# First norm of a decoder trunk: two weight chunks transferred ahead of the second and third tile of x, and split one token tile earlier

## The chip, the cores and the metric

The kernel runs on one core of one Trainium2 chip. The metric is the device time of one execution in microseconds; the time before is the median of three runs. A core has five engines, each with an instruction stream of its own that it works off in order: TensorE (PE, matrix products, into PSUM), VectorE (DVE), ScalarE (ACT), GpSimd (POOL) and SyncE (SP), which here issues all transfers between DRAM and SBUF. The engines wait for each other through semaphores.

## The reference, cut to what matters

The program is a decoder trunk of two residual layers (attention in the first, retention in the second) and a final norm, all in float32, for 512 tokens of width 1024. The change touches only the beginning: the first RMS norm of x and the first of many projections with the wide matrix `even_w_in`.

```python
def rms_norm(x, g):
    xf = x.astype(f32)
    y = xf * lax.rsqrt(jnp.mean(xf * xf, axis=-1, keepdims=True) + EPS)
    return (y * g.astype(f32)).astype(x.dtype)

def even_layer(x, g_norm, w_in, b_f, w_out):
    z = rms_norm(x, g_norm) @ w_in
    ...
    return x + y @ w_out
```

## The kernel before

The 512 tokens are four tiles of 128 (`NT`), one token to a partition, in `xres`. The width 1024 is eight tiles of 128 (`KT`).

**Products.** Each operand of a product is split into a high and a low part (line 140, `split`): ScalarE copies the value rounded to the fast matmul type, VectorE subtracts that copy from the value. A product is then three matmuls (line 210, `three`; lines 211 to 213): high by high, high by low, low by high. So TensorE's L211 needs only ScalarE's halves, L212 VectorE's half of the one operand and L213 that of the other.

**Weights.** They come in chunks of 512 KB: `load_next` (line 163) takes the next chunk of `plan` and issues its transfer into a raw buffer `w_raw`, of which there are three; `split_next` (line 170) splits the oldest loaded chunk in two halves (`w_h` on ScalarE, `w_l` on VectorE) and calls `load_next` for another. The first two chunks, 512 rows by 256 columns each, are the two halves of the first projection's weights. Here they are called w0 and w1, and the third, fourth and so on w2, w3.

**First norm.** SyncE issues the gain row, the first tile of x and the identity matrix (lines 87 to 89), then from line 707 on the other three tiles of x, with a `load_next` behind the second tile and one behind the third. TensorE spreads the gain row over the partitions (line 717) and runs a few warm-up matmuls on data of no meaning (`warm_up`, line 704). For each tile, `stats` (line 720) has ScalarE square and sum it (L723) and take the root (L724), VectorE the reciprocal (L726), and VectorE or GpSimd four small steps (L725, L727 to L730); `norm` (line 733) scales the tile in two halves on VectorE (L736); `transpose_tile` (line 148) turns it in two halves of four 128x128 blocks on TensorE (L153, `ps_xt`) and splits each half on the way out of PSUM (`xT`, on ScalarE and VectorE: "evacuation" and "low half" below). The statistics of tile t+2 are written behind the norm of tile t+1.

**What sets the order.** Inside the norm's block the instructions of ScalarE and VectorE stand among themselves as the code has them (`manual_schedule`), as GpSimd's do in the whole program. All else is placed by a scheduler, by its own estimate of when operands are ready: TensorE's and SyncE's order, and on ScalarE and VectorE what belongs to the projections, such as the split of w2, which `weights` (line 201) calls; the scheduler may set it between the norm's instructions. Each engine works through its finished list and stops at the first instruction whose data is missing.

**First projection.** `proj_tokens` with `by_tile` (line 237) goes tile by tile: for each of the four tiles 12 matmuls with w0 and 12 with w1, 96 in all, named `pt`. The next projection (`pf`, line 217) uses w2 and w3 and needs all four tiles.

Of the kernel before, what the change touches and what calls it, by code (L numbers as in the profile page):

```python
# [60 lines left out]
def trunk(ctx: ExitStack, tc, x, even_norm, even_w_in, even_b_f, even_w_out,  # L61
# [78 lines left out]
    def split(hi, lo, src, scale=1.0):  # L140

        act.activation(hi, src, AF.Copy, scale=scale)  # L142
        if isinstance(scale, float) and scale == 1.0:
            dve.tensor_tensor(lo, src, r32(hi), ALU.subtract)  # L144
        else:
            dve.scalar_tensor_tensor(lo, src, scale, r32(hi), ALU.mult, ALU.subtract)  # L146

    def transpose_tile(t, xn):
        for q in range(2):
            ps = ps_t.tile([P, 4, P], F32, tag="t", name="ps_xt")  # L150
            for k in range(4):
                kt = 4 * q + k
                pe.transpose(ps[:, k, :], xn[:, kt * P:(kt + 1) * P], ident)  # L153
            dst = xT[:, :, 4 * q:4 * q + 4, t * P:(t + 1) * P]
            split(dst[:, 0], dst[:, 1], ps)
# [7 lines left out]
    def load_next():  # L163
        if plan:
            src, *how = plan.pop(0)
            raw = wp.tile([P, src.shape[0] // P, src.shape[1]], F32, tag="raw", name="w_raw")
            dma(out=raw, in_=src.rearrange("(k p) c -> p k c", p=P))
            loaded.append((raw, *how))

    def split_next():  # L170
        if loaded:
            raw, de, tiles, kt0 = loaded.pop(0)
            shape = list(raw.shape)
            if tiles:
                h, l = tiles(shape)
            else:

                n, at = (16, 0) if de == "f" else (0, 8 if de == "v" else 0)
                h, l = (wp.tile([P, WCH], F32R, tag=tag, name=name)[:, at:at + 1024 + n * shape[1]].rearrange(
                    "p (k c) -> p k c", k=shape[1]) for tag, name in (("wh", "w_h"), ("wl", "w_l")))  # L180
            src, h_, l_ = raw, h, l
            if de == "f":
                fw = late["fw"].pop(0)
                split(h[:, :, 256:], l[:, :, 256:], fw)
                h_, l_ = h[:, :, 0:256], l[:, :, 0:256]
            elif de is True:
                src = raw.rearrange("p k (f two) -> p k two f", two=2)
                h_, l_ = (z.rearrange("p k (two f) -> p k two f", two=2) for z in (h, l))
            if kt0 is not None:
                for k in range(shape[1]):  # L190
                    split(h_[:, k], l_[:, k], src[:, k], scale=gain1[:, kt0 + k:kt0 + k + 1])
            else:
                n = shape[1] // 2
                for i in range(2):
                    sl = slice(i * n, (i + 1) * n)
                    split(h_[:, sl], l_[:, sl], src[:, sl])
            ready.append((h, l))
            count["split"] += 1
        load_next()
# [190 lines left out]
    with ExitStack() as l0:  # L390
# [311 lines left out]
        def warm_up(n, a):  # L702
            for _ in range(n):
                pe.matmul(warm, lhsT=ident, rhs=a, start=True, stop=True)

        xn = [qp.tile([P, D], F32, tag="q", name="xn") for _ in range(NT)]
        dma(out=xres[:, 1, :], in_=xsrc[:, 1, :])
        load_next()
        dma(out=xres[:, 2, :], in_=xsrc[:, 2, :])
        load_next()  # L710
        dma(out=xres[:, 3, :], in_=xsrc[:, 3, :])
        ones = ap_.tile([1, P], F32, tag="tmp", name="ones", bufs=1)
        pool.memset(ones, 1.0)
# [5 lines left out]
        with tc.manual_schedule(engines={mybir.EngineType.Activation, mybir.EngineType.DVE}):  # L719
            def stats(t, eng):  # L720

                ss, v, sd, r, e = (sm.tile([P, 1], F32, tag=n, name=n) for n in ("ss", "var", "sd", "rs", "re"))
                act.activation(xn[t], xres[:, t, :], AF.Square, accum_out=ss)  # L723
                act.activation(sd, ss, AF.Sqrt, bias=eps, scale=1.0 / D)  # L724
                eng.tensor_scalar(v, ss, 1.0 / D, EPS, ALU.mult, ALU.add)  # L725
                dve.reciprocal(r, sd)  # L726
                eng.tensor_tensor(e, r, v, ALU.mult)  # L727
                eng.tensor_tensor(e, e, r, ALU.mult)
                eng.tensor_scalar(e, e, -0.5, 1.5, ALU.mult, ALU.add)
                eng.tensor_tensor(r, r, e, ALU.mult)  # L730
                return r

            def norm(t, r):
                for h in range(2):
                    hs = slice(h * H, (h + 1) * H)
                    dve.scalar_tensor_tensor(xn[t][:, hs], xres[:, t, hs], r, gain0[h], ALU.mult, ALU.mult)  # L736

            norm(0, stats(0, dve))
            r = stats(1, pool)
            for t in range(NT):  # L740
                transpose_tile(t, xn[t])
                if t == 0:
                    warm_up(8, xn[0][:, 0:P])
                if t + 1 < NT:
                    norm(t + 1, r)
                if t < 2:
                    split_next()
                    r = stats(t + 2, pool)
        load_constants()
        for f in G[0]["proj"]:  # L750
# [179 lines left out]
```

## Time and profile before

| | |
|---|---|
| time, median of three runs | 1008.73 us (1007.95 to 1008.86) |
| the profiled execution | 1007.98 us |
| its span, first to last instruction | 1006.0 us |
| DMA, mean over the span | 99 GB/s |
| VectorE busy, share of the span | 64% |

All times inside an execution count from the start of its span. A line of the time line gives start, duration, engine, line of code, operation, output and inputs, the count of merged instructions and, in brackets, how long the engine had been idle and what ended that. A line of the waits gives the total wait in us, how often, and the longest. A line of the table by stretches gives the stretch, its length, the busy time of PE, PE's weight loads, DVE, ACT and POOL with their instruction counts, the granted clock, the share of the DMA engines and GB/s. The stage at issue is the first 30 us:

```profile
PEclk9999999999999999999999999999999999999999
DMA  7554776534556694336433223222212321332112
GB/s 207 114 138 78 156 83 104 145 97 98 135 105 111 118 94 129 77 72 134 77 103 117 74 89 122 84 84 84 84 64 84 105 83 64 87 103 84 64 42 83
```

Each digit or number stands for a fortieth of the span, 25 us; the first is the stage of the change, where transfers are at their densest.

### The profile page before, as it was taken

Reading aid. Unit: us, or ns where it says so; the run is one execution under the profiler, and the core shown is the slowest. Engines: PE = TensorE matmul, PEld = TensorE weight load, DVE = VectorE, ACT = ScalarE, POOL = GpSimd, SP = SyncE. Lnnn points to the kernel's source line nnn. Section 1 sums busy time; section 2 is a strip of 40 time slices with the busy share of each in tenths; the row PEclk is TensorE's granted clock in tenths of the full one; section 3 lists DMA queues with packets and bytes.
Section 4 is the critical chain, followed back from the end, with each engine's and each line's share of the span. In section 5 each row is a group of like instructions: output and inputs, shape, how many; then the busy total and the mean of one; then the engine's idle time right before and its main releaser. Section 6 shows DMA issues by size and latency. Waiting matters only on the chain.

```text
span 1006.0 us, 14334 instructions
## 1 busy us (share of the span) xinstructions
PE 984.2 (98%) x5150; PEld 834.5 (83%) x5150; DVE 644.5 (64%) x1427; ACT 496.9 (49%) x1029; POOL 230.9 (23%) x331
## 2 busy tenths in 40 slices
PE   8999999999999999999999999999999999999997
PEld 6888898888888988988987789787888888888875
DVE  6458576685676676666668755667547834784485
ACT  6366465555645645654658654253433343334333
POOL 1011444445344441211213100202101300130021
PEclk9999999999999999999999999999999999999999
DMA  7554776534556694336433223222212321332112
GB/s 207 114 138 78 156 83 104 145 97 98 135 105 111 118 94 129 77 72 134 77 103 117 74 89 122 84 84 84 84 64 84 105 83 64 87 103 84 64 42 83
DMA packets 74295, 99.98 MB, mean 99 GB/s; under 512 B 6369, under 2 KB 49633, under 8 KB 74098
## 3 DMA queue, kind: packets, MB, share of 16 engines
q1 hardware_dynamic: 74226, 99.09, 42.3%
q8 instruction: 40, 0.66, 0.3%
q14 instruction: 29, 0.24, 0.1%
HBM read 84.36 MB, written 2.13 MB: 86 GB/s over the span
## 4 chain that ended last, share of the span: by engine, by line
PE 85%; DVE 5%; ACT 3%; issue 2%; DMA 2%; POOL 2%; SPq 0%; DVEq 0%; POOLq 0%; ACTq 0%
PE pf L211 10%; PE pf L212 10%; PE pf L213 10%; PE po L213 6%; PE po L211 5%; PE po L212 5%; PE pw L212 5%; PE pw L213 5%; PE pw L211 5%; PE pt L211 3%; PE pt L213 3%; PE ps_pt L553 3%; PE pt L212 3%; PE ps_o L566 2%; PE ps_s L539 2%
## 5 line engine op out<-in xcount | busy, mean ns | idle before, releaser
L211 PE MATMUL pf<-xT,w_h 128*128 128x512 f32 x512 | 202.0, 394 | 0.0
L213 PE MATMUL pf<-xT,w_l 128*128 128x512 f32 x512 | 200.5, 392 | 0.0
L212 PE MATMUL pf<-xT,w_h 128*128 128x512 f32 x512 | 200.2, 391 | 0.0
L144 DVE TENSOR_TENSOR w_l<-w_raw,w_h 128x512 fp32r<-128x512 f32 x190 | 138.7, 756 | 52.9 <-ACT w_h L142 41.2
L142 ACT ACTIVATE w_h<-w_raw 128x512 fp32r<-128x512 f32 x190 | 111.9, 624 | 90.9 <-PE pf L212 40.4
L546 POOL TENSOR_SCALAR pi<-pi,st 128x512 f32<-128x512 f32 (+3 forms) x128 | 74.8, 586 | 348.6 <-DVE st L545 311.6
L213 PEld LDWEIGHTS pf<-xT,w_l 128*128 128x128 f32 x512 | 96.1, 188 | 21.0
L212 PEld LDWEIGHTS pf<-xT,w_h 128*128 128x128 f32 x512 | 96.2, 188 | 17.9
L211 PEld LDWEIGHTS pf<-xT,w_h 128*128 128x128 f32 x512 | 96.2, 188 | 17.8
L146 DVE SCALAR_TENSOR_TENSOR w_l<-w_raw,small,w_h 128x256 fp32r<-128x256 f32 (+1 forms) x136 | 86.2, 669 | 33.1 <-ACT w_h L142 32.9
L142 ACT ACTIVATE w_h<-w_raw,small 128x256 fp32r<-128x256 f32 (+1 forms) x136 | 73.0, 596 | 66.5 <-PE pw L213 24.4
L142 ACT ACTIVATE pth<-ps_pt 128x512 fp32r<-128x512 f32 (+3 forms) x128 | 55.2, 431 | 85.4 <-PE ps_pt L553 78.9
L212 PE MATMUL pw<-w_l,xT 128*128 128x512 f32 x224 | 87.3, 390 | 1.2 <-DVE w_l L146 1.2
L211 PE MATMUL pw<-w_h,xT 128*128 128x512 f32 x224 | 88.0, 393 | 0.1
L213 PE MATMUL pw<-w_h,xT 128*128 128x512 f32 x224 | 87.3, 390 | 0.0
L544 ACT ACTIVATE pi<-pi,st 128x512 f32<-128x512 f32 (+3 forms) x128 | 71.4, 558 | 27.4 <-DVE st L542 26.5
L211 PE MATMUL pt<-w_h,xT 128*128 128x256 f32 x288 | 81.5, 283 | 1.5 <-ACT w_h L142 1.5
L212 PE MATMUL pt<-w_l,xT 128*128 128x256 f32 x288 | 80.8, 280 | 0.0
L213 PE MATMUL pt<-w_h,xT 128*128 128x256 f32 x288 | 80.5, 280 | 0.0
L843 POOL TENSOR_TENSOR yn<-yn,gate 128x512 f32<-128x512 f32 x16 | 21.8, 1364 | 248.4 <-DVE yn L842 178.8
L333 DVE TENSOR_TENSOR xres<-po,xres 128x512 f32<-128x512 f32 x88 | 59.8, 683 | 26.8 <-PE po L213 26.8
L144 DVE TENSOR_TENSOR ptl<-ps_pt,pth 128x512 fp32r<-128x512 f32 (+3 forms) x128 | 62.1, 487 | 14.8 <-ACT pth L142 12.6
(185 smaller groups left out, 2019.0 us busy)
## 6 DMA issues: line engine op xcount, KB each, us to landing
w_raw<-in_even_w_in_dram SPq DMA_DIRECT2D x64, 512.0 KB, 5.6
w_raw<-in_odd_w_in_dram SPq DMA_DIRECT2D x48, 512.0 KB, 3.6
w_raw<-in_even_w_out_dram SPq DMA_DIRECT2D x16, 512.0 KB, 4.4
w_raw<-in_odd_w_out_dram SPq DMA_DIRECT2D x16, 512.0 KB, 3.5
qb<-qa SPq DMA_DIRECT2D x32, 128.0 KB, 3.0
qb<-qa SPq DMA_DIRECT2D x16, 256.0 KB, 3.2
qa<-qa SPq DMA_DIRECT2D x32, 128.0 KB, 2.5
cs<-c_dram SPq DMA_DIRECT2D x16, 256.0 KB, 3.6
```

The costliest lines, as they stand in the source:

```text
L142: act.activation(hi, src, AF.Copy, scale=scale)
L144: dve.tensor_tensor(lo, src, r32(hi), ALU.subtract)
L146: dve.scalar_tensor_tensor(lo, src, scale, r32(hi), ALU.mult, ALU.subtract)
L211: pe.matmul(ps, lhsT=ah, rhs=bh, start=first, stop=False)
L212: pe.matmul(ps, lhsT=ah, rhs=bl, start=False, stop=False)
L213: pe.matmul(ps, lhsT=al, rhs=bh, start=False, stop=last)
L333: dve.tensor_tensor(xr, ps, xr, ALU.add)
L539: pe.matmul(ps[:, 0:n], lhsT=q[:, 1, qs], rhs=k[:, 0:n], start=False, stop=True)
L544: act.activation(pi[:, 0:n], pi[:, 0:n], AF.Exp, bias=st[:, 0:1], scale=-1.0, accum_out=st[:, 1:2])
L546: pool.tensor_scalar(pi[:, 0:n], pi[:, 0:n], st[:, 2:3], 1.0, ALU.mult, ALU.mult)
L553: pe.transpose(pt[:, (i - j) * P:(i - j + 1) * P], hs["p"][i][:, j * P:(j + 1) * P], ident)
L843: pool.tensor_tensor(yn, yn, r["g"][:, i, :], ALU.mult)
```

## The change

Two edits. The two `load_next` calls move ahead of the second and the third tile of x; and the two `split_next` calls in the norm move forward: w0's split ahead of the loop, in front of tile 0's evacuation, and w1's into the loop's first pass, in front of the statistics of the third tile. The splits also carry the `load_next` calls for w2 and w3 with them.

```diff
         xn = [qp.tile([P, D], F32, tag="q", name="xn") for _ in range(NT)]
+        load_next()
         dma(out=xres[:, 1, :], in_=xsrc[:, 1, :])
         load_next()
         dma(out=xres[:, 2, :], in_=xsrc[:, 2, :])
-        load_next()
         dma(out=xres[:, 3, :], in_=xsrc[:, 3, :])
...
             norm(0, stats(0, dve))
             r = stats(1, pool)
+            split_next()
             for t in range(NT):
                 transpose_tile(t, xn[t])
                 if t == 0:
                     warm_up(8, xn[0][:, 0:P])
                 if t + 1 < NT:
                     norm(t + 1, r)
+                if t == 0:
+                    split_next()
                 if t < 2:
-                    split_next()
                     r = stats(t + 2, pool)
```

SyncE's list, the issues of the first transfers (`xres` is a tile of x, `w_raw` a weight chunk, `dil` a mask table), before and then after:

```order
L707 DMA xres<-in_x_dram 128x1024
L167 DMA w_raw<-in_even_w_in_dram 128x4x256
L709 DMA xres<-in_x_dram 128x1024
L167 DMA w_raw<-in_even_w_in_dram 128x4x256
L711 DMA xres<-in_x_dram 128x1024
L167 DMA w_raw<-in_even_w_in_dram 128x4x256
L404 DMA dil<-in_dil_dram 128x512
L167 DMA w_raw<-in_even_w_in_dram 128x4x256
```

```order
L167 DMA w_raw<-in_even_w_in_dram 128x4x256
L708 DMA xres<-in_x_dram 128x1024
L167 DMA w_raw<-in_even_w_in_dram 128x4x256
L710 DMA xres<-in_x_dram 128x1024
L711 DMA xres<-in_x_dram 128x1024
L167 DMA w_raw<-in_even_w_in_dram 128x4x256 x2
L404 DMA dil<-in_dil_dram 128x512
```

w0 and w1 have each passed one tile of x, the second and the third; w3 has passed `dil`.

ScalarE's list from the square of the second tile on (L723 a square, L724 its root, `xT` an evacuation, `w_h` half a split of a chunk), before and then after:

```order
L723 ACTIVATE xn,ss<-xres 128x1024
L724 ACTIVATE sd<-ss,small 128x1
L142 ACTIVATE xT<-ps_xt 128x4x128 x2
L142 ACTIVATE w_h<-w_raw 128x512 x2
L723 ACTIVATE xn,ss<-xres 128x1024
L724 ACTIVATE sd<-ss,small 128x1
L142 ACTIVATE xT<-ps_xt 128x4x128 x2
L142 ACTIVATE w_h<-w_raw 128x512 x2
L723 ACTIVATE xn,ss<-xres 128x1024
L142 ACTIVATE w_h<-w_raw 128x512
L724 ACTIVATE sd<-ss,small 128x1
L142 ACTIVATE w_h<-w_raw 128x512
```

```order
L723 ACTIVATE xn,ss<-xres 128x1024
L724 ACTIVATE sd<-ss,small 128x1
L142 ACTIVATE w_h<-w_raw 128x512 x2
L142 ACTIVATE xT<-ps_xt 128x4x128 x2
L142 ACTIVATE w_h<-w_raw 128x512 x2
L723 ACTIVATE xn,ss<-xres 128x1024
L724 ACTIVATE sd<-ss,small 128x1
L142 ACTIVATE xT<-ps_xt 128x4x128
L142 ACTIVATE w_h<-w_raw 128x512
L142 ACTIVATE xT<-ps_xt 128x4x128
L723 ACTIVATE xn,ss<-xres 128x1024
L142 ACTIVATE w_h<-w_raw 128x512
```

w0's split now stands ahead of the first tile's evacuation, w1's ahead of the third tile's square, and the first half of w2's, placed by the scheduler, between the two evacuations of the second tile. VectorE's low halves follow in the same order, but for the norm of the second tile, which stands ahead of w1's.

TensorE's list around the last tile's transposes (`xn_116` is that tile; `pt0` are the products of the first two tiles, `pt1` of the last two), before and then after:

```order
L213 MATMUL pt0_283<-w_h_189,xT_81 128x256
L153 MATMUL ps_xt_263<-ident_82,xn_116 128x128 x4
L211 MATMUL pt0_283<-w_h_226,xT_81 128x256
L212 MATMUL pt0_283<-w_l_227,xT_81 128x256
L153 MATMUL ps_xt_270<-ident_82,xn_116 128x128 x4
L213 MATMUL pt0_283<-w_h_226,xT_81 128x256
```

```order
L213 MATMUL pt1_284<-w_h_165,xT_81 128x256
L153 MATMUL ps_xt_263<-ident_82,xn_116 128x128 x4
L211 MATMUL pt1_284<-w_h_165,xT_81 128x256
L212 MATMUL pt1_284<-w_l_166,xT_81 128x256
L153 MATMUL ps_xt_270<-ident_82,xn_116 128x128 x4
```

Before, the last transposes stand behind 36 of the 96 `pt` matmuls, half way through the second tile's; after, behind 57, in the third tile's.

## The prediction

> **What bounds the kernel now.** I read the page first, for the engine that sets the end, then TensorE's waits, then the first 30 us instruction by instruction, since the change stays inside them.
>
> ```profile
> PE 984.2 (98%) x5150; PEld 834.5 (83%) x5150; DVE 644.5 (64%) x1427; ACT 496.9 (49%) x1029; POOL 230.9 (23%) x331
> PE 85%; DVE 5%; ACT 3%; issue 2%; DMA 2%; POOL 2%; SPq 0%; DVEq 0%; POOLq 0%; ACTq 0%
> ```
>
> TensorE (PE) is busy for 98% of the span and carries 85% of the chain that ended last. Little but TensorE's idle time can be won or lost. The table by stretches (us, then each engine's busy time and instruction count) says where that lies:
>
> ```profile
> 11.84:21.47 9.63, 7.29 (x53) 6.16 (x53) 8.67 (x17) 7.84 (x16) 2.36 (x10) 1.00 0.85 216
> 21.47:29.39 7.92, 7.92 (x69) 7.92 (x70) 4.20 (x7) 2.96 (x5) 0.00 (x0) 1.00 0.57 117
> 29.39:1003.00 973.61, 959.57 (x4994) 813.68 (x4992) 627.83 (x1395) 480.50 (x998) 227.12 (x309) 1.00 0.42 96
> ```
>
> From 11.84 (warm-up matmuls over) to 21.47 TensorE idles 2.34 of 9.63 us; from 21.47 to 29.39, when the first `pf` matmul starts, not at all; afterwards 14.04 us in 973.61, spread out. In those 9.63 us VectorE (8.67) and ScalarE (7.84) are the full ones. So the question is **when the first `pf` matmul starts**: whatever it shifts by, all behind it shifts by, as nothing later is moved by the change. Who was waited for up to 21.6 us:
>
> ```profile
> PE pt L211 <- ACT w_h L142: 1.5, 2, 0.8
> PE ps_xt L153 <- DVE xn L736: 0.7, 1, 0.7
> ```
>
> Two waits on a weight split, one on a normalised tile. The change aims at the first two; the price is paid by the tiles.
>
> **Landings.** I write x1, x2, x3 for the second to fourth tile of x, w0, w1, w2 for the weight chunks. SyncE's issues (start, us), then the time from issue to landing, of the same five in that order:
>
> ```profile
> 2.01 0.43 SPq L707 DMA_DIRECT2D xres<-in_x_dram  x1
> 2.49 0.43 SPq L167 DMA_DIRECT2D w_raw<-in_even_w_in_dram  x1
> 2.96 0.51 SPq L709 DMA_DIRECT2D xres<-in_x_dram  x1
> 3.51 0.43 SPq L167 DMA_DIRECT2D w_raw<-in_even_w_in_dram  x1
> 3.99 1.76 SPq L711 DMA_DIRECT2D xres<-in_x_dram  x1
> ```
>
> ```profile
> xres<-in_x_dram SPq DMA_DIRECT2D x1, 512.0 KB, 4.8
> w_raw<-in_even_w_in_dram SPq DMA_DIRECT2D x1, 512.0 KB, 9.4
> xres<-in_x_dram SPq DMA_DIRECT2D x1, 512.0 KB, 10.1
> w_raw<-in_even_w_in_dram SPq DMA_DIRECT2D x1, 512.0 KB, 11.1
> xres<-in_x_dram SPq DMA_DIRECT2D x1, 512.0 KB, 11.9
> ```
>
> They land at 6.8 (x1), 11.9 (w0), 13.1 (x2), 14.6 (w1) and 15.9 (x3): in the order of issue. All are 512 KB, yet w0 came 5.1 us after x1 and x2 only 1.2 after w0.
>
> **The change, part by part.** No instruction and no byte is added or removed. Three things move.
>
> (1) x1 goes behind w0, x2 behind w1. x0 landed at about 4.7 (first row below). If w0 keeps its 5.1 us it lands at 9.8, and x1 1.2 later, as x2 did: **11.0**. Bounds: late, 11.9, where the pair w0 and x1 as a whole was done before; early, 7.5, when each takes no longer than x3 behind w1 (1.3 to 1.4 us). I take 11.0, nearest to how w0 itself behaved. w1 then lands 1.5 behind x1 or later, by 13.3; x2 by 14.6, x3 at 15.9, w2 behind x3 at about 17.2 (by 17.54 in any case, where its split ran): the same five in front of the same place.
>
> (2) On ScalarE the square of x1 stands ahead of everything else and now waits 4 us longer. Queued behind it: both halves of w0's split, tile 0's evacuation, w1's split, the square of x2. ScalarE's rows of before give the steps:
>
> ```profile
> 4.70 1.06 ACT L723 ACTIVATE xn<-xres 128x1024 f32<-128x1024 f32 x1 [2.48 <-DMA xres<-in_x_dram]
> 6.87 1.06 ACT L723 ACTIVATE xn<-xres 128x1024 f32<-128x1024 f32 x1 [0.63 <-DMA xres<-in_x_dram]
> 13.11 1.06 ACT L723 ACTIVATE xn<-xres 128x1024 f32<-128x1024 f32 x1
> 14.50 1.06 ACT L142 ACTIVATE xT<-ps_xt 128x512 fp32r<-128x512 f32 x2
> 15.46 1.15 ACT L142 ACTIVATE w_h<-w_raw 128x512 fp32r<-128x512 f32 x2
> 16.50 1.05 ACT L723 ACTIVATE xn<-xres 128x1024 f32<-128x1024 f32 x1
> 17.54 0.62 ACT L142 ACTIVATE w_h<-w_raw 128x512 fp32r<-128x512 f32 x1
> 18.06 0.28 ACT L724 ACTIVATE sd<-ss,small 128x1 f32<-128x1 f32 x1
> ```
>
> Start to start: square with its root 1.39 (13.11 to 14.50), two evacuations 0.96, two split halves 1.04, a half 0.52. After: square x1 11.0, w0 12.4, tile 0 13.4, w1 14.4, square x2 15.4 (before 13.11, where x2's landing held it), free at 16.8. Tile 1's two evacuations now stand on both sides of w2's first half, so the square of x3 follows at about 18.5 (before 16.50) and its root at 18.5 + 1.56 = 20.0 (before 18.06). The chain of tile 3 is 2.0 us late on ScalarE.
>
> (3) VectorE's order follows, and there the delay is met by slack. Its rows, with the last step on GpSimd:
>
> ```profile
> 13.09 1.29 DVE L144 TENSOR_TENSOR w_l<-w_raw,w_h 128x512 fp32r<-128x512 f32 x2
> 14.62 0.17 DVE L726 RECIPROCAL rs<-sd 128x1 f32<-128x1 f32 x1 [0.25 <-ACT sd L724]
> 15.76 0.19 POOL L730 TENSOR_TENSOR rs<-rs,re 128x1 f32<-128x1 f32 x1
> 15.11 1.29 DVE L144 TENSOR_TENSOR xT<-ps_xt,xT 128x512 fp32r<-128x512 f32 x2 [0.32 <-ACT xT L142]
> 16.32 1.40 DVE L736 SCALAR_TENSOR_TENSOR xn<-xres,rs,gain 128x512 f32<-128x512 f32 x2
> 17.63 1.28 DVE L144 TENSOR_TENSOR w_l<-w_raw,w_h 128x512 fp32r<-128x512 f32 x2
> 20.59 1.40 DVE L736 SCALAR_TENSOR_TENSOR xn<-xres,rs,gain 128x512 f32<-128x512 f32 x2
> ```
>
> Two low halves take 1.21 start to start (15.11 to 16.32), a norm 1.31 (16.32 to 17.63), reciprocal to end of GpSimd's steps 1.33 (14.62 to 15.95). After: w0's low halves from 13.0 to 14.2, tile 0's to 15.4, norm 1 to 16.7, w1's to 17.9, reciprocal of tile 2, tile 1's low halves to 19.3, norm 2 (GpSimd done 19.3) to 20.6, reciprocal of tile 3, GpSimd done 22.0, w2's first low half and tile 2's to 22.8, norm 3 at **22.8** against 20.59. Its first half lets the last tile's transposes start at 22.8 + 0.88 = **23.7**, against 21.47, 2.2 us late. What TensorE has done by then decides:
>
> ```profile
> 6.05 2.50 PE L704 MATMUL warm<-ident 128*128 128x128 f32 x10
> 10.34 1.50 PE L704 MATMUL warm<-xn,ident 128*128 128x128 f32 x12
> 16.14 0.39 PE L211 MATMUL pt<-w_h,xT 128*128 128x256 f32 x1 [0.76 <-ACT w_h L142]
> 21.47 0.63 PE L153 MATMUL ps_xt<-ident,xn 128*128 128x128 f32 x4
> 22.73 0.28 PE L211 MATMUL pt<-w_h,xT 128*128 128x256 f32 x1
> 29.39 0.40 PE L211 MATMUL pf<-xT,w_h 128*128 128x512 f32 x1
> ```
>
> From 22.73 to 29.39 run 57 `pt` matmuls, 0.117 each. Before, TensorE stood at the last transposes with 36 of the 96 `pt` matmuls done; 60 and the 8 transposes took 7.92 us, so the transposes cost 0.90. After, the order of TensorE's instructions puts them behind 57: 24 of tile 0, 24 of tile 1 and 9 of tile 2. These can be done: w0 and w1 are both split when tile 1's low half is there (18.8), tile 1's first 12 end at 20.2, the third tile's transposes and the other 12 by 22.5, tile 2's 9 by 23.6. So 39 are left: 23.7 + 39 x 0.117 + 0.90 = **29.2** against 29.39. The two weight waits go, TensorE works instead of standing, and the last tile's delay eats the win: **-0.2 us** by this hand count. Half a step of rounding sits in several places; I take -0.3.
>
> Edits at nothing, with the rows that cover them:
>
> ```profile
> 7.86 1.28 SPq L404 DMA_DIRECT2D dil<-in_dil_dram  x1
> 28.19 1.15 ACT L142 ACTIVATE w_h<-w_raw 128x512 fp32r<-128x512 f32 x2 [3.60 <-PE pt L213]
> ```
>
> The fourth chunk, w3, is still issued when w0's low halves are done (13.09 + 1.29 = 14.4 before, 14.2 after), and its split stands at 28.19 waiting for TensorE to free a buffer, not for data. The mask tables (`dil`, 7.86) now queue behind w3, so some 7 us later; the softmax reads them first, behind the projections that start at 29.39. Were that cover gone, those 7 us at most would be the price.
>
> **Rivals.**
> *Transfers come early* (w0 is not the slow one, only the one that caught a slow stretch). Each microsecond x1 gains is a microsecond of ScalarE until w2's landing takes over as the late one: w2's first half stands between tile 1's evacuations, so the square of x3 cannot start before 17.2 + 1.0 = 18.2. With that x1 is worth 0.3 to 0.6 more, -0.9 in all; w2 early as well, x2's landing at 14.6 is the next bound, 0.8 ahead of the 15.4 above: -1.1, and with the roundings of the walk -1.6 at most. For it: x2 and x3 took 1.2 to 1.4 us. Against: 1.5 us or more for every w chunk, and w0's 5.1. 1007.1 to 1007.8 us.
> *x1 later than 11.9*, since SyncE already stalls 1.76 us in issuing x3 and w0's transfer may slow in front. Nothing is hidden then, 1:1: x1 at 12.5 gives +1.1, 13 gives +1.6: 1009.2 to 1010.3.
> *TensorE slows down in the longer gap* (the slower side). Ten warm-up rows took 2.50 us at 6.05, twelve took 1.50 at 10.34: 0.250 then 0.125 each, so TensorE starts at half speed and was fast by 10.34. Before, the longest idle behind that was 0.76 us (16.14) and the 57 matmuls behind it run at full pace. After, it idles from 11.84 until tile 0's first evacuation, 13.4 + 0.6 = 14.0: 2.2 us, three times what this trace shows to be harmless; with x1 at 11.9, 3.1. If the speed halves again for the 3.7 us (6.05 to about 9.7) it took to rise, 1.8 us are lost, twice that for 7.4 us: +1.5 to +3.4 with the forecast's -0.3, 1010.2 to 1012.1. It decides from x1 at about 12 on, where the gap reaches some 3.2 us. The Trainium skill, "TensorE: Matmul & The Clock Gate", part 1 on the clock gate, puts the drop to half clock after at least one idle window of about 3.4 us in free-running windows; by that rule 2.2 us is safe and only the late x1 is not. The trace agrees with the halved start and shows no drop; a gap of over 0.76 us is not in it.
> *The change does nothing to the order* is out: the instruction orders differ as described.
>
> **How the numbers follow.** The profiled execution took 1007.98 us for its span of 1006.0. Its sum is 1007.98 - 0.3 = 1007.7. The median of the three runs is 0.75 above it, so on that scale 1008.73 - 0.3 = 1008.4. Forecast (x1 at 10.4 to 11.9, -0.8 to +0.5): chance 0.62, 1007.9 to 1009.2. Early: 0.16. Later x1: 0.12. Slow TensorE: 0.08; the rest elsewhere. The range takes in the early case and the late one, with the 0.45 that the runs shown differ from their middle: 1006.8 to 1010.2. About 0.2%, 2.0 us, is what a measurement of this kernel can tell from no change; only the slow TensorE, or an early case beyond its bound, leaves that band: faster 0.05, same 0.85, slower 0.10.
>
> **What would show it.** In the profile after: x1's square starting at 10.4 to 11.9; no wait of TensorE on `w_h`; the square of x3 near 18.5 right behind tile 1's second evacuation; norm 3 near 22.8, the last transposes 0.9 later with 57 matmuls ahead of them; `pf` first at 28.6 to 29.9. Wrong if x1's square starts before 9, if `pt` matmuls are over 0.2 us apart, if the first `pf` matmul moves by more than 1.6 us, or if it moves and the end does not.

## The result and the profile after

| | before | after |
|---|---|---|
| median of 20 runs each | 1008.40 us (1007.44 to 1011.30) | 1011.34 us (1008.29 to 1012.59) |
| ratio | | 1.0021, 95% interval 1.0014 to 1.0028 |
| the profiled execution, its span | 1007.98, 1006.0 us | 1011.96, 1010.0 us |
| first `pf` matmul in that span | 29.39 us | 32.64 us |

The change made the kernel slower, by 0.2%, and the interval leaves out no change. The forecast of 1008.4 us was wrong, and the median lies 1.1 us above its range. The page of the changed kernel first, its lines on the engines' busy time and on the chain that ended last:

```profile
PE 985.3 (98%) x5150; PEld 836.9 (83%) x5150; DVE 644.7 (64%) x1427; ACT 496.5 (49%) x1029; POOL 231.2 (23%) x331
PE 85%; DVE 4%; ACT 4%; issue 2%; DMA 2%; POOL 2%; SPq 0%; DVEq 0%; POOLq 0%; ACTq 0%
```

The page gives nothing away: every share is within a point of what it was before. TensorE is busy for 1.1 us more (985.3 against 984.2) with as many instructions, so some ran slower, and the other 2.9 us of the longer span are idle time. Where, the waits of TensorE between 5 and 34 us tell:

```profile
PE pt L211 <- ACT xT L142: 4.0, 1, 4.0
PE pt L213 <- DVE xT L144: 0.4, 1, 0.4
```

The two waits on a weight split (`w_h`) and the one on a normalised tile are gone, the first two as the change meant; one wait of 4.0 us on the first tile's evacuation has come instead. The reason stands in the transfers. SyncE's issues of w0 (L167) and x1 (L708), and the time from issue to landing of w0, x1, w1 and x2 in that order:

```profile
2.01 0.43 SPq L167 DMA_DIRECT2D w_raw<-in_even_w_in_dram  x1
2.49 0.51 SPq L708 DMA_DIRECT2D xres<-in_x_dram  x1
```

```profile
w_raw<-in_even_w_in_dram SPq DMA_DIRECT2D x1, 512.0 KB, 9.9
xres<-in_x_dram SPq DMA_DIRECT2D x1, 512.0 KB, 10.7
w_raw<-in_even_w_in_dram SPq DMA_DIRECT2D x1, 512.0 KB, 12.1
xres<-in_x_dram SPq DMA_DIRECT2D x1, 512.0 KB, 12.9
```

w0 was issued 0.48 us earlier than before and landed at 2.01 + 9.9 = 11.9, when it had landed before too (2.49 + 9.4). Being first in the queue brought it nothing. x1, now behind it, came 1.25 us later still, at 13.2 instead of 6.8. ScalarE's time line behind that:

```profile
13.21 1.06 ACT L723 ACTIVATE xn<-xres 128x1024 f32<-128x1024 f32 x1 [6.89 <-DMA xres<-in_x_dram]
14.59 1.13 ACT L142 ACTIVATE w_h<-w_raw 128x512 fp32r<-128x512 f32 x2
15.63 1.06 ACT L142 ACTIVATE xT<-ps_xt 128x512 fp32r<-128x512 f32 x2
16.59 1.14 ACT L142 ACTIVATE w_h<-w_raw 128x512 fp32r<-128x512 f32 x2
17.63 1.05 ACT L723 ACTIVATE xn<-xres 128x1024 f32<-128x1024 f32 x1
20.55 0.60 ACT L142 ACTIVATE xT<-ps_xt 128x512 fp32r<-128x512 f32 x1 [1.46 <-PE ps_xt L153]
22.04 1.06 ACT L723 ACTIVATE xn<-xres 128x1024 f32<-128x1024 f32 x1
```

ScalarE stands for 6.89 us before the square of x1, with w0's split and tile 0's evacuation queued behind it. And TensorE's time line:

```profile
10.80 1.50 PE L704 MATMUL warm<-xn,ident 128*128 128x128 f32 x12
16.26 0.38 PE L211 MATMUL pt<-w_h,xT 128*128 128x256 f32 x1 [3.95 <-ACT xT L142]
17.75 0.42 PE L213 MATMUL pt<-w_h,xT 128*128 128x256 f32 x1
17.96 0.42 PE L211 MATMUL pt<-w_h,xT 128*128 128x256 f32 x1
19.46 1.75 PE L153 MATMUL ps_xt<-ident,xn 128*128 128x128 f32 x8
21.17 0.28 PE L213 MATMUL pt<-w_h,xT 128*128 128x256 f32 x1
21.29 0.28 PE L211 MATMUL pt<-w_h,xT 128*128 128x256 f32 x1
32.64 0.40 PE L211 MATMUL pf<-xT,w_h 128*128 128x512 f32 x1
```

From 17.75 on the `pt` matmuls stand 0.21 us apart, at 21.17 only 0.12: a stretch at half speed. The table by stretches, cut where the clock changes, shows it (stretch, length, busy PE, weight loads, DVE, ACT, POOL, then the granted clock):

```profile
10.68:14.10 3.42, 1.63 (x15) 1.43 (x13) 0.00 (x0) 0.89 (x1) 0.00 (x0) 1.00 0.87 301
14.10:17.51 3.41, 0.82 (x4) 0.62 (x5) 2.44 (x5) 3.38 (x9) 1.76 (x5) 1.00 0.37 139
17.51:20.92 3.41, 3.41 (x18) 3.41 (x17) 2.81 (x6) 1.92 (x5) 0.56 (x3) 0.50 0.93 176
20.92:24.33 3.41, 3.41 (x32) 3.41 (x31) 2.83 (x6) 2.97 (x7) 0.58 (x4) 1.00 0.89 144
32.64:1007.00 974.36, 959.44 (x4994) 814.03 (x4992) 628.10 (x1395) 480.27 (x998) 226.79 (x309) 1.00 0.42 96
```

The clock falls to 0.50 at 17.51, behind 3.41 us in which TensorE was busy for 0.82, and rises again 3.41 us later. The profile of before holds 1.00 from 9.74 on. Behind the first `pf` matmul little differs: from there to the end of the span it is 977.3 us (1009.97 less 32.64) against 976.6 before (1006.02 less 29.39), and one transfer wait at 119 us is 0.67 us longer than before. So 3.25 of the 4.0 us of span are lost before the first `pf` matmul, by two causes that follow from each other: a late x1, and a gap long enough to cost the clock.

One more thing is needed to read the times. They fall in two groups. Of the 20 of before, 15 lie between 1007.4 and 1008.9 us (their median 1008.18), 5 above 1010.1 (1010.70). Of the 20 after, the five with a mean clock of 0.998 or 0.999 have a median of 1008.89, the fifteen with 0.994 to 0.997 one of 1011.71. A window of 3.41 us at half clock takes 0.5 x 3.41 / 1010 = 0.0017 off the mean clock, so in the changed kernel the group with the shorter times is the one that kept the clock. For the 20 of before no clock is on record: that their two groups are the same is inferred from their times. The mean clock is a rough mark. Every profile also has half clock over its last 1.9 to 4.5 us, which is 0.0009 to 0.0022 of the mean, and the record of the clock starts only when it first rises.

### The profile page after: what moved, and what is told of

It is laid out like the page before. It is cut to its first block, busy times and chain, and to the rows that moved or that the text cites. A ratio compares the mean times of both kernels' runs of the same rounds, so it can differ in the third digit from the quotient of the medians.

```text
span 1010.0 us, 14334 instructions
## 1 busy us (share of the span) xinstructions
PE 985.3 (98%) x5150; PEld 836.9 (83%) x5150; DVE 644.7 (64%) x1427; ACT 496.5 (49%) x1029; POOL 231.2 (23%) x331
## 4 chain that ended last, share of the span: by engine, by line
PE 85%; DVE 4%; ACT 4%; issue 2%; DMA 2%; POOL 2%; SPq 0%; DVEq 0%; POOLq 0%; ACTq 0%
PE pf L211 10%; PE pf L212 10%; PE pf L213 10%; PE po L213 5%; PE po L211 5%; PE po L212 5%; PE pw L212 5%; PE pw L213 5%; PE pw L211 5%; PE pt L213 3%; PE pt L211 3%; PE pt L212 3%; PE ps_pt L553 3%; PE ps_o L566 2%; PE ps_s L539 2%
## 5 line engine op out<-in xcount | busy, mean ns | idle before, releaser
L212 PEld LDWEIGHTS pf<-xT,w_h 128*128 128x128 f32 x512 | 96.3, 188 | 17.6
```

The costliest lines, as they stand in the source:

```text
L212: pe.matmul(ps, lhsT=ah, rhs=bl, start=False, stop=False)
```

## The experiments

Each kernel was timed beside the kernel before. "Kept" below means executions with a mean clock of at least 0.998, "lost" those under it.

**1. The changed kernel again, and with more warm-up.** The second has 16 warm-up matmuls behind the first tile, to fill the gap ahead of the first `pt` matmul:

```diff
                 if t == 0:
-                    warm_up(8, xn[0][:, 0:P])
+                    warm_up(16, xn[0][:, 0:P])
```

> The changed kernel once more, unaltered, beside the kernel before, for the granted clock of each execution. Theory 'gate': TensorE stands idle for 3.4 us or more between the warm-up matmuls and the first pt matmul, its clock is halved for one or two stretches of 3.4 us, and that costs. Then executions with a mean granted clock of 0.999 are within +0.0 to +1.0 us of before, those with 0.994 to 0.997 are +1.5 to +4 us. Theory 'landing': x1, behind w0, lands later than predicted (13.2 us in the profile against 11.0), and ScalarE's list is late by that; then the time is +1 to +2 us whatever the clock says.

> The changed kernel with eight more warm-up matmuls (16 for 8) behind the first tile's transposes: some 2.0 us more of TensorE work in a gap of 4 us (eight at two rows of 0.125). No byte and no order of ScalarE and VectorE changes. Gate: the idle stretch falls to some 2 us, the granted clock is 0.999 in every execution, no pt matmul is over 0.2 us apart, and the time falls by 1.0 to 1.5 us against the changed kernel. Landing: the time stays within 0.3 us of the changed kernel's; the square of x1 still waits for x1 until 11 to 13 us.

The changed kernel: 1012.18 us (1011.34 to 1012.83), ratio 1.0024 (1.0015 to 1.0033), lost in all 9 executions; x1's square at 13.65, gap 4.23 us. With the fill: 1011.82 us, 1.0017 (1.0005 to 1.0029). The fill left a gap of 0.93 us in its profile, which is of an execution that kept the clock, but 9 of 12 lost it all the same, so as a cure it missed. The three that kept it took 1008.86 to 1009.08, the nine others 1009.6 to 1013.85. Beside them the kernel before kept it in 19 of 30 (median 1009.18) and lost it in 11 (1010.84). As no execution of the first kernel kept the clock, it shows only one of the two groups that the theories tell apart (2.2 us above the median of before, 1010.0). The profile of the second helps, since it has the order of the change and a held clock. Its square of x1, its norm of tile 3 and its first `pf` matmul:

```profile
12.26 1.06 ACT L723 ACTIVATE xn<-xres 128x1024 f32<-128x1024 f32 x1 [5.78 <-DMA xres<-in_x_dram]
24.10 1.40 DVE L736 SCALAR_TENSOR_TENSOR xn<-xres,rs,gain 128x512 f32<-128x512 f32 x2
30.44 0.39 PE L211 MATMUL pf<-xT,w_h 128*128 128x512 f32 x1
```

From x1's square to the first `pf` matmul are 18.18 us, 19.43 in the profile of the change. So of the 3.25 us that the change loses up to there, **1.25 come with the lower clock and 2.0 with the late x1**.

**2. One half of the change at a time.** Splits moved, transfers as before; and transfers moved, splits as before (both against the kernel before):

```diff
+            split_next()
             for t in range(NT):
...
+                if t == 0:
+                    split_next()
                 if t < 2:
-                    split_next()
                     r = stats(t + 2, pool)
```

```diff
+        load_next()
         dma(out=xres[:, 1, :], in_=xsrc[:, 1, :])
         load_next()
         dma(out=xres[:, 2, :], in_=xsrc[:, 2, :])
-        load_next()
```

> The splits one tile further forward, the transfers in the order of before. x1's square is back at 6.9 us; w0's split waits for w0 (11.9) ahead of the first tile's evacuation. Gate: the first pt matmul comes at 13.6 us, a gap of 1.8 us, so the clock stays at 0.999. Landing: the chain of the third tile starts at 15.7 (behind w1's split, 14.6 + 1.0) and not at 17.6, the first pf matmul at 28.5 us against 29.4 before. Both theories: -0.4 to -1.2 us against before. If the early splits themselves were the harm: slower than before by 1 us or more.

> The transfers of the change, the splits where they were before. The square of x1 waits for x1 (11 to 13 us), and the first tile's evacuation, w0's split and the square of x2 stand behind it. First pt matmul at 14.1 (x1 at 11.0) to 16.3 us (x1 at 13.2), first pf matmul at 30.9 to 33.1 us. Landing: +1.5 to +3.6 us against before, as much as or more than the whole change. Gate: with a gap of 2.3 to 4.5 us the clock falls in some executions, which are then +2.5 to +4. If the transfers' order were harmless: within 0.5 us of before.

The splits alone: 1009.49 us, ratio 1.0000 (0.9991 to 1.0009), first `pf` at 29.64, the clock lost in 6 of 11 executions; both theories had expected 0.4 to 1.2 us of gain and a first `pf` at 28.5, and both missed. The transfers alone: 1012.37 us, 1.0024 (1.0014 to 1.0034), first `pf` at 34.15, lost in all 8 executions. So **the order of the transfers is the whole loss**, and the order of the splits is worth nothing that can be measured. The stretches of the second show the clock falling behind an idle window and staying at half for two:

```profile
12.65:16.06 3.41, 0.00 (x0) 0.00 (x0) 0.55 (x2) 2.35 (x6) 0.58 (x3) 1.00 0.83 298
16.06:19.47 3.41, 2.29 (x10) 2.03 (x10) 3.41 (x7) 3.02 (x7) 1.02 (x3) 0.50 0.26 94
19.47:22.89 3.42, 3.42 (x18) 3.42 (x17) 3.26 (x7) 3.17 (x8) 1.16 (x5) 0.50 0.66 117
```

**3. The other way round: all tiles of x ahead of the weights.** Both kernels issue x1, x2, x3 and only then w0, w1 and w2. They differ in how far the splits go back:

```diff
         dma(out=xres[:, 1, :], in_=xsrc[:, 1, :])
-        load_next()
         dma(out=xres[:, 2, :], in_=xsrc[:, 2, :])
-        load_next()
         dma(out=xres[:, 3, :], in_=xsrc[:, 3, :])
+        load_next()
+        load_next()
...
                 if t < 2:
-                    split_next()
                     r = stats(t + 2, pool)
+                if 0 < t < 3:
+                    split_next()
```

```diff
                 if t < 2:
-                    split_next()
                     r = stats(t + 2, pool)
+                    split_next()
```

> All three tiles of x are transferred ahead of the three weight chunks, and the splits of the chunks stand behind the squares of the next tile. What it tells apart is what the first weight chunk's landing hangs on. Theory A (the first chunk lands at about 12 us whatever stands ahead of it, because one DMA engine's share of it is late): x1, x2 and x3 land at about 6.8, 8 and 9.5, the first chunk at 12 to 12.5, the other two within 3 us behind; no square waits for a tile after 10 us, the first pf matmul moves from 29.4 to 26 to 28, and the time is 1.5 to 3 us below the kernel before. Theory B (the chunk takes 5 to 7 us from the landing ahead of it): the first chunk lands at 14 to 16.5, the first pt matmul waits till about 17 to 19, TensorE's gap grows to 5 us or more, and the time is 1 to 4 us above the kernel before.

> The same order of transfers as the run beside it, but only the squares of the second and third tile are moved ahead of a split; every split keeps its step. Theory A (first chunk at about 12 us in any case): the first pf matmul at 27 to 29 and a time 0.5 to 2 us below the kernel before. Theory B (first chunk 5 to 7 us behind the landing ahead of it, 14 to 16.5 us): the first pf matmul at 31 or later and a time 1 to 4 us above.

x1, x2 and x3 landed at 8.0, 9.3 and 10.6 us in the first, w0 at 13.3; in the second w0 at 14.0. That is neither "12 in any case" nor 5 to 7 us behind the tile ahead (2.8 and 3.1 were measured). The times: 1010.47 us, 1.0012 (1.0003 to 1.0021), lost in all 12 executions; and 1008.62 us, 0.9993 (0.9985 to 1.0002), kept in all 12. Neither gain of theory A arrived. Nor did its earlier `pf`: in the first kernel the scheduler set one `pf` matmul, at 23.30, ahead of 70 of the `pt` matmuls, and the next starts at 31.81; in the second the first starts at 29.88. The first version waits 2.16 us for a norm at 16.47 and loses the clock behind a window with 1.25 us of busy:

```profile
14.00:17.41 3.41, 1.25 (x11) 0.99 (x10) 3.08 (x6) 3.32 (x8) 0.96 (x5) 1.00 0.75 163
17.41:20.83 3.42, 3.42 (x17) 3.09 (x16) 3.42 (x7) 3.11 (x6) 1.19 (x4) 0.50 0.54 79
```

**4. The clock by itself: the kernel before with 14 and with no warm-up matmuls behind the first tile.**

```diff
-                    warm_up(8, xn[0][:, 0:P])
+                    warm_up(14, xn[0][:, 0:P])
```

```diff
-                    warm_up(8, xn[0][:, 0:P])
+                    warm_up(0, xn[0][:, 0:P])
```

> The kernel before with 14 matmuls of warm-up behind the first tile instead of 8, so TensorE stands idle only some 0.1 us or so ahead of the first pt matmul. Theory (the clock falls when a window of 3.41 us has less than about half of it busy, and the kernel before loses it in a part of its executions, by where the window falls): every execution shows a clock of 0.998 to 0.999 and 1007.4 to 1009.5 us, the kernel before beside it again spreads up to 1011 or more, ratio 0.998 to 0.9995. Rival (the slower executions of the kernel before have another cause than the idle stretches in its first 20 us): the spread of this kernel is that of the kernel before, clocks of 0.996 to 0.999, ratio 0.9995 to 1.0005.

> The kernel before without the 8 matmuls of warm-up behind the first tile: the transfers, the splits and everything else stay where they were. It prices a lost clock by itself. Theory (the lower clock behind the idle stretch is worth 1.2 us or more by itself): half clock in the windows from about 13 to 20 us in every execution, pt matmuls about 0.21 us apart in part of them, the first pf matmul 1 to 2.5 us later than in the kernel before, a time of 1010.5 to 1012.5 and ratio 1.001 to 1.0025. Rival (the late x1 is the whole loss of the change, the lower clock runs beside other waits and costs nothing): the first pf matmul within 0.5 us of the kernel before, ratio 0.9995 to 1.0005.

With 14: 1009.15 us, 0.9999 (0.9990 to 1.0008), and 4 of 11 lost it: the theory's "every execution" missed, and the ratio is the rival's. But the fill doesn't reach the later gaps. The profiled one lost it behind the next gap, of 1.33 and 0.68 us on w1's split and tile 2's norm:

```profile
16.05:19.46 3.41, 1.60 (x10) 1.11 (x10) 3.34 (x6) 3.41 (x9) 1.30 (x5) 1.00 0.93 226
19.46:22.87 3.41, 3.41 (x17) 3.41 (x17) 3.40 (x7) 1.38 (x3) 0.77 (x4) 0.50 0.84 121
```

Without warm-up: 1010.38 us, 1.0008 (0.9999 to 1.0018), below the theory's 1.001 to 1.0025 and above the rival's. The yardstick was badly chosen, since the kernel before itself lost the clock in 14 of the 35 executions beside it (median 1010.38) and kept it in 21 (1008.84). By its mean clock the kernel without warm-up lost it in 10 of 11, and the eleventh, the profiled one with 0.999, did not have it either: its `pt` matmuls stand 0.21 us apart up to 18.8 us, where the record of its clock begins, and its first `pf` matmul starts at 30.43, 1.04 later than in the profile of before. So this kernel, with the order of its transfers untouched, takes as long as the executions of before that lost the clock and 1.5 us longer than those that kept it. An estimate of what a lower clock costs here is thus about 1.5 us.

**5. Twice the suspected cost, and none of it.** First w1, too, ahead of x1; then the changed kernel with x1 issued by ScalarE, whose first instruction it becomes, so that it doesn't stand in SyncE's queue behind w0 (both against the changed kernel):

```diff
         load_next()
-        dma(out=xres[:, 1, :], in_=xsrc[:, 1, :])
         load_next()
+        dma(out=xres[:, 1, :], in_=xsrc[:, 1, :])
```

```diff
-        dma(out=xres[:, 1, :], in_=xsrc[:, 1, :])
+        nc.scalar.dma_start(out=xres[:, 1, :], in_=xsrc[:, 1, :])
```

> The changed kernel with the second weight chunk, too, issued ahead of the second tile of x: the order is w0, w1, x1, x2, x3, w2, the splits as in the change. It doubles the suspected cost. Theory (all of the loss comes from the landing of x1, ahead of which ScalarE does nothing): x1 lands one transfer later, at 14 to 15.5 us instead of 12.2 to 13.7, its square follows at once, TensorE's gap ahead of the first pt matmul grows to 5 to 6.5 us, the clock is lost in every execution (0.994 to 0.997), the first pf matmul starts at 33.5 to 36, and the ratio to the kernel before is 1.003 to 1.005 against the 1.0021 to 1.0024 of the change. Rival (the loss comes from the new places of the splits or from the weight chunks, not from x1): w1 earlier helps or changes nothing, ratio 1.0015 to 1.0025.

> The changed kernel, but the transfer of x1 is issued by ScalarE at the start of the program, so it does not stand behind w0 in SyncE's queue; w0, w1, x2, x3 keep their order there, the splits stay as in the change. Theory (x1 is late only because it stands behind w0's packets in the same queue): x1 lands by 9 us and w0 by 12.5, the square of x1 starts by 9, TensorE's gap ahead of the first pt matmul falls below 2.5 us, the first pf matmul starts at 28.5 to 30, and the ratio to the kernel before is 0.999 to 1.0003, like that of the splits alone. Rival (the DMA engines, not the queue, hold x1 up: what is in flight by then keeps them full): x1 lands at 11 to 13.5 as in the change, ratio 1.0015 to 1.003.

w1 ahead as well: 1014.50 us, ratio 1.0056 (1.0043 to 1.0069), more than the theory's 1.003 to 1.005 and in its direction. Three rows of it, x1's square, the first `pt` and the first `pf` matmul:

```profile
16.41 1.06 ACT L723 ACTIVATE xn<-xres 128x1024 f32<-128x1024 f32 x1 [10.05 <-DMA xres<-in_x_dram]
```

```profile
19.45 0.58 PE L211 MATMUL pt<-w_h,xT 128*128 128x256 f32 x1 [7.46 <-ACT xT L142]
...
35.75 0.40 PE L211 MATMUL pf<-xT,w_h 128*128 128x512 f32 x1
```

Against the profile of the change x1's square is 3.20 us later and the first `pf` matmul 3.11: **one to one**, as nothing hides a late x1 any more (both profiles have a stretch at half clock, one window in the change, two here, the first of them mostly idle). With x1 issued by ScalarE the loss goes: 1009.22 us, 1.0002 (0.9992 to 1.0011), 9 of 11 kept. The transfer's issue, then the square of x1, right behind that of the first tile, and w0's split:

```profile
0.72 0.38 ACTq L708 DMA_DIRECT2D xres<-in_x_dram  x1
...
6.93 1.04 ACT L723 ACTIVATE xn<-xres 128x1024 f32<-128x1024 f32 x1
...
9.81 1.16 ACT L142 ACTIVATE w_h<-w_raw 128x512 fp32r<-128x512 f32 x2 [1.42 <-DMA w_raw<-in_even_w_in_dram]
```

x1 landed at 4.2 us. It was issued earlier, at 0.72 instead of 2.49, and beside SyncE's queue; which of the two it owes the landing to, this run doesn't separate. w0 was issued where the change has it, and the other transfers kept their order; the first `pf` matmul starts at 29.36. So with x1 early the splits and the early w0 cost nothing that can be measured.

**6. Why is w0 slow?** w0 goes in rows of 1 KB, x1 in rows of 4 KB. The kernel before, with x1 in four pieces of 1 KB rows, puts short rows of another tensor where the change has w0:

```diff
-        dma(out=xres[:, 1, :], in_=xsrc[:, 1, :])
+        for k in range(4):
+            dma(out=xres[:, 1, k * 256:(k + 1) * 256], in_=xsrc[:, 1, k * 256:(k + 1) * 256])
```

> The kernel before, with x1 transferred in four pieces of 256 columns, so that its 512 KB go in rows of 1 KB, as those of the weight chunks do, instead of rows of 4 KB. x1 then stands where w0 stands in the change, first behind x0, with w0's row length. It asks why w0 took 6 to 7.6 us in that place, where x1 takes 2 to 4. Theory A (the short rows): the last piece of x1 lands 5.5 to 7.6 us behind x0, at 10.5 to 12.5 us, its square starts there, w0 lands at 12.5 to 14.5, the first pf matmul starts 1.5 to 3.5 us later than in the kernel before, ratio 1.001 to 1.0025. Theory B (the weight tensor's memory, whose first rows are slow to read whatever stands ahead): the last piece of x1 lands at 6.8 to 9.3 us, w0 at 11.9 to 13.2 as in the kernel before, ratio 0.9995 to 1.001.

x1's last piece landed at 8.3 us, as theory B had it: short rows alone aren't slow there. But w0, issued at 3.91, landed at 14.2 and not at 11.9 to 13.2, so B missed too in that number. 1010.04 us, 1.0005 (0.9997 to 1.0014); the first `pf` matmul at 32.74, in a profile that lost the clock. The numbers of all profiles side by side say what neither theory had (SyncE's issue of w0, from issue to landing, landing, in us):

| kernel | transferred ahead of w0, behind x0 | issue | takes | lands |
|---|---|---|---|---|
| the change, four profiles | nothing | 2.01 to 2.02 | 9.0 to 10.3 | 11.0 to 12.4 |
| w1 ahead of x1, too | nothing | 2.01 | 10.3 | 12.3 |
| x1 issued by ScalarE | nothing in its queue | 2.01 | 7.8 | 9.8 |
| before, and three with its transfers | x1 | 2.48 to 2.49 | 9.4 to 10.4 | 11.9 to 12.9 |
| x1 in four pieces | x1 | 3.91 | 10.3 | 14.2 |
| the version of part 7 | x1, x2 | 2.96 | 9.2 | 12.2 |
| all of x first, two kernels | x1, x2, x3 | 3.43 to 3.44 | 9.9 to 10.5 | 13.3 to 14.0 |

But for one kernel, **w0 lands 9.0 to 10.5 us behind its issue, whatever is transferred ahead of it**: none, one, two or three tiles (only the order of the change and that of before have more than two profiles).

The traces say more. A transfer's semaphore is counted up in sixteen marks, by the reading of the trace one for each DMA engine's share, and the transfer has landed with the last. These are the times of four of w0's marks:

| kernel | ahead | 8th | 12th | 15th | 16th |
|---|---|---|---|---|---|
| the change | nothing | 7.02 | 7.87 | 9.49 | 11.94 |
| before | x1 | 9.05 | 9.44 | 10.09 | 11.87 |
| the version of part 7 | x1, x2 | 10.01 | 10.91 | 12.18 | 12.21 |
| all of x first, first kernel | x1, x2, x3 | 11.47 | 11.74 | 13.09 | 13.33 |

Half of w0 comes the earlier the less stands ahead of it: over all profiles the 8th mark lies at 6.5 to 7.5 us with nothing ahead, at 8.9 to 9.5 behind one tile, at 10.0 behind two, at 10.9 and 11.5 behind three. It is the last few shares that come late, by up to 5.8 us behind the 8th mark. So the change did bring most of w0 forward by some 2 us, and one late share undid it; x1's sixteen marks in the change follow w0's at 1.2 to 1.3 us each, the late one too. Why these shares are late isn't shown by any of these runs and stays open.

**7. A version that beats both.** If w0 takes some 10 us from its issue whatever goes ahead, the tiles of x that fit into them are free. x1 and x2 stand ahead of w0, x3 behind it, and the statistics ahead of the splits (against the kernel before):

```diff
         dma(out=xres[:, 1, :], in_=xsrc[:, 1, :])
-        load_next()
         dma(out=xres[:, 2, :], in_=xsrc[:, 2, :])
         load_next()
         dma(out=xres[:, 3, :], in_=xsrc[:, 3, :])
+        load_next()
...
                 if t < 2:
-                    split_next()
                     r = stats(t + 2, pool)
+                    split_next()
```

> A version that may beat both: x1 and x2 ahead of w0, x3 behind it, then w1 and w2; the squares of the second and third tile stand ahead of the splits. Theory (the first chunk lands the later the more stands ahead of it, but by less than those transfers take: 12 to 12.5 us in front of x1, 11.9 to 12.9 behind x1, 13.3 to 14 behind all three tiles): x2 lands at 9 to 9.7, w0 at 12.5 to 13.3, the first pt matmul starts at 13.5 to 14.5, no wait of over 1.5 us on TensorE behind the warm-up, clock 0.998 to 0.999 in nearly all executions, the first pf matmul at 28 to 29.5, and the ratio to the kernel before is 0.9985 to 0.9995. Rival (VectorE, which is full there, sets the last transposes whatever lands first): the first pf matmul at 29.4 to 30 and ratio 0.9995 to 1.0005.

1008.04 us (1007.00 to 1008.73), ratio 0.9986 (0.9977 to 0.9995): faster than the kernel before and, by the ratios, than the change. x2 landed at 8.8 us and w0 at 12.2, both earlier than the theory had them. Its waits of TensorE up to 34 us, and its first `pf` matmul:

```profile
PE pt L211 <- ACT w_h L142: 1.1, 1, 1.1
PE ps_xt L153 <- DVE xn L736: 0.4, 1, 0.4
PE pt L211 <- ACT xT L142: 0.3, 1, 0.3
```

```profile
29.38 0.40 PE L211 MATMUL pf<-xT,w_h 128*128 128x512 f32 x1
```

That is where the profile of before has it (29.39), and its span of 1006.1 us is that of before too, so the start of `pf` gained nothing, nearly as the rival had it. Most of the gain lies elsewhere: all 11 executions kept the clock, while the kernel before lost it in 10 of the 21 beside them (median 1010.63, against 1008.54 for those that kept it).

## Why the prediction was wrong

**What bounds the kernel: right.** All that moved, moved through the start of the first `pf` matmul, but for 0.67 us of a later transfer wait.

**(1) Landings: the step that failed.** The prediction let w0 keep "its 5.1 us" behind the transfer ahead of it and put x1 at 11.0, with 11.9 as the late bound. w0 took 7.2 us behind x0 (11.94 less 4.75) and x1 landed at 13.2; in the other profiles of the changed order that keep x1 next behind w0 it landed at 12.2 to 13.7. Most of w0 did move up, its 8th mark from 9.05 to 7.02, but the landing is the last mark, and that stayed (11.87 and 11.94). The quoted rows held the better constant, 9.4 us from issue to landing: w0's issue moves by only 0.48 us, so its landing hardly moves. The bound failed for the same reason, as it took w0 and x1 to be done as a pair when they were before; the group as a whole came later too, x3 at 17.6 us instead of 15.9. "x1 1.2 later" than w0 was right (1.25).

**(2) ScalarE: right once x1's landing is put in.** From x1's square to tile 0's evacuation 2.4 us were predicted, 2.42 came (13.21 to 15.63); to the square of x2 4.4 and 4.42. The square of x3 came 8.8 us behind instead of 7.5, as ScalarE waited 1.46 us for transposes at half speed; with the clock held (the profile of part 1 with the fill, 12.26 to 19.73) it came 7.5 behind.

**(3) VectorE and TensorE: the sum was sized for a held clock.** The norm of tile 3 was put 11.8 us behind x1's square:

```profile
26.29 1.40 DVE L736 SCALAR_TENSOR_TENSOR xn<-xres,rs,gain 128x512 f32<-128x512 f32 x2
```

It came 13.1 us behind. The first `pf` matmul, put at 29.2, came at 32.64: of the 3.4 us, 2.2 are x1's delay over 11.0 and 1.2 the clock. With the clock held the sum was right: in the profile with the fill the norm came 11.8 us behind x1's square, and `pf` 18.2, as predicted (29.2 less 11.0). Edits at nothing (w3, the mask tables) cost nothing that shows: the one later wait that grew, at 119 us, is on another transfer.

**Rivals: two came true together, at too low a chance.** "x1 later than 11.9" had 0.12, "TensorE slows down in the longer gap" 0.08. The second was priced at 1010.2 to 1012.1 us, from x1 at 12 and a gap of 3.2 us on; x1 came at 13.2, the gap was 3.95, the median 1011.34. The mechanism and the price were right; the chance hung on the landing in (1). Its condition asked for too much: the clock is lost with gaps of 1.33 and 0.68 us in one window (part 4), well short of one of 3.2. Two of the prediction's own signs of being wrong came: `pt` matmuls over 0.2 us apart, and a first `pf` matmul moved by more than 1.6 us (3.25).

**The scale was off as well.** The three runs shown, 1007.95 to 1008.86, had all kept the clock by their times; they are the first of the 20, and five of the 17 others had not. "The trace shows no drop" held for one execution. Taken by groups, the change costs 0.7 us where the clock is kept (1008.18 to 1008.89), 1.0 where it is lost (1010.70 to 1011.71), and moves half of all executions from the one to the other, 2.5 us apart: 0.5 x 2.5 + 0.25 x 0.7 + 0.75 x 1.0 = 2.2 us, 0.0022 of the time, where the ratio has 0.0021. By that count 1.25 of the 2.2 us are executions that lose the clock which didn't before. The share is not firm: in part 1 the kernel before had already lost the clock in 11 of 30, its groups were 1.7 us apart, and the same count gives 0.63 x 1.7 = 1.1 of 2.4 us. The groups aren't the same in all else either: an execution that loses the clock may do so because its transfers were late, and no run here separates the two within one kernel.

## What to carry to other kernels

For a transfer near the start of a kernel read the time from its issue, not only the time behind the transfer ahead of it: if the first hardly varies, moving the transfer up the queue gains the few tenths of its issue and delays all that it passes. A transfer has landed when its last share has, so a queue's order moves most of it and may still not move the landing. Before a gap on TensorE is made longer, see how near the kernel is to losing its clock: look at the mean clock of every run shown, not of the profiled one alone, and count a version that always keeps it as a gain even where its best time is no better. Where the engine that evacuates works in order, put ahead of its work only what lands first.

## What the runs showed of the hardware

**The clock falls without an idle window.** It fell behind windows of 3.41 us with TensorE busy for 0.00 (the transfers alone), 0.82 (the change), 1.25, 1.43 (the change again) and 1.60 us (counting the windows back from the changes of the clock); it held behind 1.63 us (the change, 10.68 to 14.10) and behind the windows of 1.96 us and more. In the kernel with x1 in four pieces it held behind 1.53 and fell behind 1.64. So the limit lies at some 45 to 48% of a window by this measure, with some blur, as the ends of matmuls are modelled. Once down it stayed at half behind a window with 2.29 us busy (67%) and rose behind 3.30 and more. The Trainium skill, "TensorE: Matmul & The Clock Gate", part 1 on the clock gate, speaks of at least one idle window of about 3.4 us: the length agrees, 3.41 between the changes here, while "idle" has to be read as less than about half busy.

**Two queues share the DMA engines.** With x1 issued by ScalarE, the first tile, issued by SyncE 0.4 us later, was there for its square at 5.48 us instead of 4.78, and x1 by 6.93. The Trainium skill, "DMA: Bandwidth & Descriptors", section on queues, rings and completion order, says that SyncE and ScalarE each have a ring on each of the same 16 DMA engines, which take turns between the rings they have work for; a first tile that comes 0.7 us later beside a second transfer agrees with that.

**The last shares of the first chunk of the weights come late.** w0 takes 9.0 to 10.5 us from its issue (7.8 once) while the 8th of its sixteen marks is there after 4.5 to 8.0 us; the transfers behind it land 1.2 to 2.8 us apart (4.1 once), and rows of 1 KB alone aren't the reason. The cause stays open.
